# Two inner layer norms in a fixed order, scaled by token and then by feature, and a residual load that waits for x

## The chip, the cores and the metric

The kernel runs on one core of one Trainium2 chip. The engines named below are PE (TensorE, matrix products), DVE (VectorE), ACT (ScalarE), POOL (GpSimd) and SP (SyncE, which only issues DMAs here). The metric is the device time of one execution in microseconds (us); the median of the runs shown is 1940.43.

## What is computed

One layer over 256 tokens of width 2048 in 32-bit floats: a half-weight gated FFN, a mixer and a second half-weight FFN, each with a residual and a layer norm behind it.

```python
def layer_norm(x, gain, bias):
    mu = jnp.mean(xf, axis=-1, keepdims=True)
    var = jnp.mean(jnp.square(xf - mu), axis=-1, keepdims=True)
    return ((xf - mu) * lax.rsqrt(var + LN_EPS)).astype(x.dtype) * gain + bias

def swiglu_ffn(x, w_gate, w_up, w_down):
    return (jax.nn.silu(x @ w_gate) * (x @ w_up)) @ w_down
...
        x = layer_norm(DEEPNORM_ALPHA * x + FFN_RES_WEIGHT * swiglu_ffn(x, ...), ln1_gain, ln1_bias)
        mix = hybrid_mixer(x, positions, ...)
        x = layer_norm(DEEPNORM_ALPHA * x + mix, ln2_gain, ln2_bias)
        x = layer_norm(DEEPNORM_ALPHA * x + FFN_RES_WEIGHT * swiglu_ffn(x, ...), ln3_gain, ln3_bias)
```

The two inner norms are the first two: what they give is both the input of the next stage, needed with features on the partitions, and the residual of the next norm, needed with tokens on the partitions.

## The kernel before, in words

The 256 tokens are two tiles t of 128. Every matrix product is done with both operands split into a high and a low part. A weight unit is 128 x 2048 values, 1 MB: SP loads it into `raw` (three buffers), ACT casts the high part `h...` (L72, four buffers), DVE subtracts the low part `l...` (L73, four buffers), and PE multiplies: three matmuls of 512 columns for each k and t where the activation is the stationary side (`mm_t`, L94 to L98), or a pair of 512 and 256 columns where the weight is (`mm_f`, L90 to L92).

The stages run in this order. The first FFN has eleven hidden slices in chunks of 4, 4 and 3; its first gate and up products (`first`, L143 to L179) load x itself, in nine pieces `xr` on ACT's DMA queue (L163), split into `x_0` to `x_3` with four k each, and the first weights on SP (L167). The residual, x with tokens on the partitions, is loaded whole into `res[0]` and `res[1]` on POOL's queue (L180, L181). After each chunk `down` adds its product to `res` in four column slices n. In the last chunk (`f1dz_p`; in the mixer the output projection `opp`) the last slice n = 3 is computed for t = 0 and then for t = 1, and the norm follows.

`LN.finish(t)` (L282 to L297) does all on DVE: aggregate the moments, the root in 11 short operations on 128 x 1 values (`rsqrt`), then for each of four slices two passes over `res`: subtract the mean and multiply by the gain (L292), multiply by the root and add the bias (L294). `LN.turn(t, n)` transposes four 128 x 128 blocks on PE into a bank (L304), ACT casts the high part (L308), DVE subtracts the low part (L309). `LN.enter` (L311 to L324) runs the first product of the next stage (`v` of the mixer, `f2s` of the second FFN) over four units and both t, with the turns between. In trace rows the first inner norm is `f1n`, the second `mxn`, the last `f2n`; `res_75` and `res_76` are `res[0]` and `res[1]`. Behind the first norm come the mixer's `xb` products, 12 blocks of 16 pairs, and then `dtp` (L458).

Each engine runs its instructions in order. That order is made by a scheduler at build time, with its own idea of durations; only the loads on POOL that are marked `keep_in_program_order` are fixed among themselves. So the short steps of the root, the passes over `res` and the weight subtractions are mixed on DVE as the scheduler judged.

Of the kernel before, what the change touches and what calls it, by code (L numbers as in the profile page):

```python
# [8 lines left out]
F32 = mybir.dt.float32  # L9
# [37 lines left out]
def tile_layer(ctx, tc, aps, out):  # L47
# [19 lines left out]

    ident = const.tile([P, P], F32, name="ident")
    make_identity(nc, ident)

    def split(raw, hi, lo):
        nc.scalar.copy(out=hi, in_=raw)  # L72
        nc.vector.tensor_tensor(out=lo, in0=raw, in1=hi.bitcast(F32), op=ALU.subtract)  # L73

    def wunit(src, name, k, c, fine=1):
# [4 lines left out]
        if fine == 1:  # L80
            nc.sync.dma_start(out=raw[:, :n], in_=src)
        for j in range(fine):
            sl = slice(j * n // fine, (j + 1) * n // fine)
            if fine > 1:
                nc.sync.dma_start(out=raw[:, sl], in_=src[:, sl])
            split(raw[:, sl], hi[:, sl], lo[:, sl])
        return (hi[:, :n].rearrange("p (k c) -> p k c", c=c),
                lo[:, :n].rearrange("p (k c) -> p k c", c=c))

    def mm_f(ps, w, act, k, first, last):  # L90
        nc.tensor.matmul(ps, lhsT=w[0][:, k, :], rhs=act, start=first, stop=False)
        nc.tensor.matmul(ps[:, :T], lhsT=w[1][:, k, :], rhs=act[:, :T], start=False, stop=last)  # L92

    def mm_t(ps, act, t, w, k, first, last):  # L94
        ah, al = act(t)
        nc.tensor.matmul(ps, lhsT=ah, rhs=w[0][:, k, :], start=first, stop=False)  # L96
        nc.tensor.matmul(ps, lhsT=ah, rhs=w[1][:, k, :], start=False, stop=False)  # L97
        nc.tensor.matmul(ps, lhsT=al, rhs=w[0][:, k, :], start=False, stop=last)  # L98
# [7 lines left out]
    def fold(ps, name):  # L106
        lo = tmp(name + "c")
        nc.scalar.copy(out=lo, in_=ps[:, T:])
        s = tmp(name + "s")
        nc.vector.tensor_tensor(out=s, in0=ps[:, :T], in1=lo, op=ALU.add)  # L110
        return s

    def rsqrt(dst, hv, shape, name):
        y = dst
        nc.vector.tensor_scalar(out=y.bitcast(I32), in0=hv.bitcast(I32), scalar1=1, scalar2=None,
                                op0=ALU.arith_shift_right)
        nc.vector.tensor_scalar(out=y.bitcast(I32), in0=y.bitcast(I32), scalar1=-1,
                                scalar2=0x5EF759DF - (1 << 31), op0=ALU.mult, op1=ALU.add)
        t = small(name + "n", shape)
        for _ in range(3):  # L120
            nc.vector.tensor_tensor(out=t, in0=y, in1=y, op=ALU.mult)
            nc.vector.tensor_tensor(out=t, in0=t, in1=hv, op=ALU.mult)
            nc.vector.scalar_tensor_tensor(out=y, in0=t, scalar=1.5, in1=y,
                                           op0=ALU.subtract, op1=ALU.mult)
# [63 lines left out]
    nc.vector.tensor_copy(out=ustr_r, in_=ustr)  # L188
# [5 lines left out]
    tc.keep_in_program_order(nc.gpsimd.dma_start(out=rows, in_=aps["rows"].broadcast_to([P, 3, SH])))  # L194

# [18 lines left out]
    def turn(toks, name, hs):  # L214
        for b2 in range(2):
            pt = bank(f"{name}T{b2}")
            for bb in range(2):
                c0 = (2 * b2 + bb) * P
                for t in range(2):
                    nc.tensor.transpose(pt[:, bb * T + t * P:bb * T + (t + 1) * P], toks[t][:, c0:c0 + P], ident)  # L220
            hi = page(f"{name}h{b2}", F32R)
            lo = page(f"{name}l{b2}", F32R)
            nc.scalar.copy(out=hi, in_=pt)
            nc.vector.tensor_tensor(out=lo, in0=pt, in1=hi.bitcast(F32), op=ALU.subtract)
# [3 lines left out]
    def add_res(ps, t, n, start):  # L228
        r = res[t][:, n * NS:(n + 1) * NS]
        nc.vector.scalar_tensor_tensor(out=r, in0=r, scalar=ALPHA if start else 1.0, in1=ps,  # L230
                                       op0=ALU.mult, op1=ALU.add)

    def down(src, act, nu, name, start, ln=None, mid=None):
        for n in range(4):
            if ln is None or n < 3:
                pss = [bank(f"{name}p{n}{t}") for t in range(2)]
                for u in range(nu):
                    w = wunit(src(n, u), f"{name}{n}_{u}", 4, NS)
                    for k in range(4):
                        kk = 4 * u + k  # L240
                        for t in range(2):
                            mm_t(pss[t], act[kk], t, w, k, kk == 0, kk == 4 * nu - 1)
                    if mid is not None and n == 0 and u == 0:
                        mid()
                for t in range(2):
                    add_res(pss[t], t, n, start)
                    if ln is not None:
                        ln.stat(t, n)
                continue
            ws = [wunit(src(n, u), f"{name}{n}_{u}", 4, NS) for u in range(nu)]  # L250
            for t in range(2):
                ps = bank(f"{name}p{n}{t}")
                for u in range(nu):
                    if t == 1 and u == nu - 1:
                        ln.turn(0, 0)
                    for k in range(4):
                        kk = 4 * u + k
# [592 lines left out]
```

## Time and profile before

| | |
|---|---|
| median of 3 runs (lowest, highest) | 1940.43 us (1940.17, 1942.39) |
| profiled execution, its own time | 1940.14 us |
| its span in the trace | 1938.4 us |
| mean granted clock of PE | 0.989 |
| PE busy | 1888.9 us, 97% |
| DVE busy | 1046.6 us, 54% |
| ACT busy | 744.1 us, 38% |
| POOL busy | 59.7 us, 3% |

The span is the time between the first and the last instruction of the trace; 1.7 us of the execution lie outside. PE's share is the mean over stages: in the long ones it is full, and its idle time lies in a few places, which the views of waits, of windows and of single instructions show. The granted clock is given as a share of the full 2.4 GHz.

### The profile page before, as it was taken

The page shows a single profiled execution, that of the slowest core. Times are in us where ns is not written, and L with a number is a line of the kernel's source. Part 1 is how long each engine was busy: PE and PEld are TensorE (multiplying, and loading weights), DVE is VectorE, ACT ScalarE, POOL GpSimd, SP SyncE. Part 2 cuts the span into 40 slices and gives each one's busy share as a digit, 9 for nine tenths or more (in the row PEclk, how much of TensorE's full clock was granted, in tenths as well). Part 3 has the DMA queues.
Part 4 walks back from the last instruction along what each step waited for, and adds up shares of the span by engine and source line. Part 5 has one row for each costly group of instructions (what it writes and reads, how often), then busy time and mean ns, then how long its engine had stood idle before and what let it go on. Part 6 is the DMA issues. An engine that isn't in the chain of part 4 may idle for free.

```text
span 1938.4 us, 20670 instructions
## 1 busy us (share of the span) xinstructions
PE 1888.9 (97%) x8722; PEld 1570.8 (81%) x8722; DVE 1046.6 (54%) x1040; ACT 744.1 (38%) x592; POOL 59.7 (3%) x69
## 2 busy tenths in 40 slices
PE   7999999999999997999999997999999999999997
PEld 6888888888888886888888885888888888888885
DVE  5544444444444456667877656544444444444456
ACT  4433333334333332553335432443333334333331
POOL 2000000000000000002400000000000000000000
PEclk9999999999999998999999998999999999999998
DMA  8655555555556553544346552555555555556551
GB/s 296 231 185 186 194 195 195 178 191 195 195 203 218 191 195 120 195 174 160 145 152 209 204 196 88 215 183 187 195 195 195 186 186 193 195 192 226 190 196 65
DMA packets 53549, 363.04 MB, mean 187 GB/s; under 512 B 6224, under 2 KB 6496, under 8 KB 10960
## 3 DMA queue, kind: packets, MB, share of 16 engines
q1 hardware_dynamic: 49536, 350.25, 50.7%
q0 software_dynamic: 2624, 9.38, 1.4%
q10 hardware_dynamic: 1296, 2.10, 0.3%
q8 instruction: 68, 1.11, 0.2%
q14 instruction: 25, 0.20, 0.0%
HBM read 359.60 MB, written 2.10 MB: 187 GB/s over the span
## 4 chain that ended last, share of the span: by engine, by line
PE 95%; DVE 2%; DMA 2%; ACT 0%; issue 0%; DVEq 0%; ACTq 0%
PE f2u L97 4%; PE f2u L98 4%; PE f2u L96 4%; PE f1g L98 4%; PE f2g L98 4%; PE f2g L97 4%; PE f1g L97 4%; PE f1u L98 4%; PE f2g L96 4%; PE f1g L96 4%; PE f1u L97 4%; PE f1u L96 4%; PE f2d_p L97 3%; PE f2d_p L96 3%; PE f1d_p L97 3%; PE f1d_p L98 3%
## 5 line engine op out<-in xcount | busy, mean ns | idle before, releaser
L73 DVE TENSOR_TENSOR lf2u<-rf2u,hf2u 128x2048 fp32r<-128x2048 f32 x44 | 100.9, 2293 | 142.4 <-ACT hf2u L72 142.4
L73 DVE TENSOR_TENSOR lf1u<-rf1u,hf1u 128x2048 fp32r<-128x2048 f32 x40 | 91.7, 2293 | 121.5 <-ACT hf1u L72 121.5
L73 DVE TENSOR_TENSOR lf2g<-rf2g,hf2g 128x2048 fp32r<-128x2048 f32 x40 | 91.7, 2293 | 101.7 <-ACT hf2g L72 101.7
L73 DVE TENSOR_TENSOR lf1g<-rf1g,hf1g 128x2048 fp32r<-128x2048 f32 x40 | 91.6, 2292 | 97.7 <-ACT hf1g L72 97.7
L97 PE MATMUL f2u<-lf2u,mxnx 128*128 128x512 f32 x352 | 137.0, 389 | 1.1 <-DVE lf2u L73 1.1
L96 PE MATMUL f2u<-hf2u,mxnx 128*128 128x512 f32 x352 | 136.6, 389 | 0.7 <-ACT hf2u L72 0.7
L98 PE MATMUL f2u<-hf2u,mxnx 128*128 128x512 f32 x352 | 136.9, 389 | 0.0
L72 ACT CAST hf2u<-rf2u 128x2048 fp32r<-128x2048 f32 x44 | 84.1, 1910 | 118.0 <-PE f2g L98 105.1
L72 ACT CAST hf2g<-rf2g 128x2048 fp32r<-128x2048 f32 x40 | 76.5, 1913 | 131.9 <-PE f2u L98 101.6
L96 PE MATMUL f1g<-hf1g,x 128*128 128x512 f32 x320 | 125.3, 392 | 0.0
L96 PE MATMUL f2g<-hf2g,mxnx 128*128 128x512 f32 x320 | 125.3, 392 | 0.0
L98 PE MATMUL f2g<-hf2g,mxnx 128*128 128x512 f32 x320 | 124.6, 389 | 0.0
L72 ACT CAST hf1g<-rf1g 128x2048 fp32r<-128x2048 f32 x40 | 76.4, 1913 | 125.4 <-PE f1u L98 95.3
L98 PE MATMUL f1g<-hf1g,x 128*128 128x512 f32 x320 | 124.6, 389 | 0.0
L97 PE MATMUL f2g<-lf2g,mxnx 128*128 128x512 f32 x320 | 124.6, 389 | 0.0
L97 PE MATMUL f1g<-lf1g,x 128*128 128x512 f32 x320 | 124.5, 389 | 0.0
L96 PE MATMUL f1u<-hf1u,x 128*128 128x512 f32 x320 | 124.5, 389 | 0.0
L97 PE MATMUL f1u<-lf1u,x 128*128 128x512 f32 x320 | 124.5, 389 | 0.0
L98 PE MATMUL f1u<-hf1u,x 128*128 128x512 f32 x320 | 124.5, 389 | 0.0
L73 DVE TENSOR_TENSOR lf2d<-rf2d,hf2d 128x2048 fp32r<-128x2048 f32 x32 | 73.4, 2293 | 85.6 <-ACT hf2d L72 85.6
L73 DVE TENSOR_TENSOR lf1d<-rf1d,hf1d 128x2048 fp32r<-128x2048 f32 x32 | 73.4, 2293 | 85.6 <-ACT hf1d L72 85.6
L72 ACT CAST hf1u<-rf1u 128x2048 fp32r<-128x2048 f32 x40 | 76.4, 1910 | 105.0 <-PE f1g L98 104.2
(817 smaller groups left out, 4358.8 us busy)
## 6 DMA issues: line engine op xcount, KB each, us to landing
rf2u<-f_u SPq DMA_DIRECT2D x44, 1024.0 KB, 4.8
rf1g<-f_g SPq DMA_DIRECT2D x40, 1024.0 KB, 4.8
rf1u<-f_u SPq DMA_DIRECT2D x40, 1024.0 KB, 4.8
rf2g<-f_g SPq DMA_DIRECT2D x40, 1024.0 KB, 4.8
rf1d<-f_d SPq DMA_DIRECT2D x32, 1024.0 KB, 4.8
rf2d<-f_d SPq DMA_DIRECT2D x32, 1024.0 KB, 4.8
rop<-wout SPq DMA_DIRECT2D x16, 1024.0 KB, 4.8
rf1dz<-f_d SPq DMA_DIRECT2D x12, 1024.0 KB, 4.8
```

The costliest lines, as they stand in the source:

```text
L72: nc.scalar.copy(out=hi, in_=raw)
L73: nc.vector.tensor_tensor(out=lo, in0=raw, in1=hi.bitcast(F32), op=ALU.subtract)
L96: nc.tensor.matmul(ps, lhsT=ah, rhs=w[0][:, k, :], start=first, stop=False)
L97: nc.tensor.matmul(ps, lhsT=ah, rhs=w[1][:, k, :], start=False, stop=False)
L98: nc.tensor.matmul(ps, lhsT=al, rhs=w[0][:, k, :], start=False, stop=last)
```

## The change

1. **A fixed order.** A flag `strict` and a thin wrapper `Ordered` around the vector, scalar and tensor engines: whatever is issued while the flag is set keeps the order of the program among itself. All helper operations of the changed kernel carry the wrapper's line, L78.
2. **The inner norms.** `LN.close` replaces the last slice of `down`, `finish` and `enter`, and writes out the order by hand: matmuls, turns, weight units (`new`) and norm steps. After the root, `shift` makes -mean x root; `hat(t, n)` scales one slice of `res` on ACT by these two values per token. `turn` transposes it; four ACT operations of 128 x 128 apply gain and bias, which are now per partition (a new constant `lnp`), into a page `l1f` or `l2f`; cast and subtraction follow from that page. Gain and bias are applied to `res` itself afterwards, in 16 operations on DVE, outside the fixed order, with broadcast loads that are issued later.
3. **The last norm.** `close_last` keeps both passes on DVE, with the four first passes put between the steps of the root.
4. **The residual load.** It stands behind the constants on POOL's queue, and a copy of one value of the last slice of x into `res[t]` precedes each load, so that the load waits for that slice.

The core of the diff:

```diff
+    strict = [False]
+    class Ordered:
...
+                ins = fn(*args, **kw)
+                return tc.keep_in_program_order(ins) if strict[0] else ins
...
-    for t in range(2):
-        tc.keep_in_program_order(nc.gpsimd.dma_start(out=res[t], in_=aps["x"][t]))
...
+    lnp = const.tile([P, 4, KD], F32, name="lnp")
+    tc.keep_in_program_order(nc.gpsimd.dma_start(out=lnp, in_=aps["lnp"]))
+    for t in range(2):
+        tc.keep_in_program_order(nc.gpsimd.tensor_copy(out=res[t][:, :1], in_=x0_4[3][:, 3, 1, T - 1:].bitcast(F32)))
+        tc.keep_in_program_order(nc.gpsimd.dma_start(out=res[t], in_=aps["x"][t]))
...
+        def shift(self, t):
+            nb = self.nb[t] = small(f"{self.name}{t}nb", (P, 1))
+            vec.scalar_tensor_tensor(out=nb, in0=self.mv[t][:, 0:1], scalar=-1.0, in1=self.rs[t],
+                                     op0=ALU.mult, op1=ALU.mult)
+
+        def hat(self, t, n):
+            sca.activation(self.part(t, n), self.part(t, n), AF.Identity, bias=self.nb[t], scale=self.rs[t])
...
+            xf = page(f"{self.name}f{t}{n}")
+            for b in range(4):
+                c = 4 * n + b
+                sca.activation(xf[:, b * P:(b + 1) * P], pt[:, b * P:(b + 1) * P], AF.Identity,
+                               bias=lnp[:, 2 * self.idx + 1, c:c + 1], scale=lnp[:, 2 * self.idx, c:c + 1])
...
-            src = pt.rearrange("p (b c) -> p b c", b=4)
-            nc.scalar.copy(out=hi, in_=src)
-            nc.vector.tensor_tensor(out=lo, in0=src, in1=hi.bitcast(F32), op=ALU.subtract)
+            src = xf.rearrange("p (b c) -> p b c", b=4)
+            sca.copy(out=hi, in_=src)
+
+            def low():
+                vec.tensor_tensor(out=lo, in0=src, in1=hi.bitcast(F32), op=ALU.subtract)
+            return low
...
+        def close(self, piece, nu, name, start):
...
+            for _ in range(4 - nu):
+                new()()
+            strict[0] = True
+            pd = [bank(f"{name}p3{t}") for t in range(2)]
+            for u in range(nu):
+                piece(pd[0], 0, u)
+            add_res(pd[0], 0, 3, start)
+            self.stat(0, 3)
+            self.moments(0)
+            self.root(0)
+            self.shift(0)
+            piece(pd[1], 1, 0)
+            low = new()
+            self.hat(0, 0)
+            self.hat(0, 1)
+            low()
+            for u in range(1, nu - 1):
+                piece(pd[1], 1, u)
+                if u < nu - 2:
+                    new()()
+            piece(pd[1], 1, nu - 1, (0, 1))
+            low = self.turn(0, 0)
+            piece(pd[1], 1, nu - 1, (2, 3))
+            low()
+            new()()
+            low = self.turn(0, 1)
+            self.hat(0, 2)
+            low()
+            add_res(pd[1], 1, 3, start)
+            self.stat(1, 3)
+            self.moments(1)
...
+            enter(0, 0)
+            low = self.turn(0, 2)
+            self.hat(0, 3)
+            low()
+            new()()
+            self.root(1)
+            self.shift(1)
+            enter(0, 1)
+            low = self.turn(0, 3)
+            self.hat(1, 0)
+            self.hat(1, 1)
+            low()
+            enter(0, 2)
+            low = self.turn(1, 0)
+            self.hat(1, 2)
+            low()
...
+            strict[0] = False
+            self.affine()
+            for n in range(4):
+                for t in range(2):
+                    r = self.part(t, n)
+                    vec.tensor_tensor(out=r, in0=r, in1=self.gb[0][n], op=ALU.mult)
+                    vec.tensor_tensor(out=r, in0=r, in1=self.gb[1][n], op=ALU.add)
+            return pe
...
+                self.root(t, [lambda n=n: first(n) for n in range(4)])
```

The built order at three places. First, ACT's queue at the start, before (`xr` is a piece of x on its way in, `x_0` its high part, `hfirstu` and `hfirstg` the high parts of the first weights):

```order
12 L163 DMA xr_259<-xT 128x512
13 L163 DMA xr_261<-xT 128x512
14 L163 DMA xr_339<-xT 128x512
15 L163 DMA xr_341<-xT 128x512
16 L72 CAST x_0_77<-xr_111 128x2x256
17 L72 CAST hfirstu_88<-rfirstu_90 128x512
18 L72 CAST x_1_78<-xr_179 128x2x256
```

and the same stretch of ACT's queue after the change:

```order
12 L194 DMA xr_259<-xT 128x512
13 L78 CAST x_0_77<-xr_111 128x2x256
14 L194 DMA xr_261<-xT 128x512
15 L78 CAST hfirstu_88<-rfirstu_90 128x512
16 L194 DMA xr_339<-xT 128x512
17 L194 DMA xr_341<-xT 128x512
18 L78 CAST x_1_78<-xr_179 128x2x256
```

The casts of `x_0` and `hfirstu` have moved ahead of the last two or three loads of x.

Second, POOL's queue at the start after the change (before, the two `res` loads stood ahead of `ltri`, with no copies):

```order
10 L212 DMA ltri<-ltri 128x128
11 L214 DMA ustr<-ustr 128x128
12 L218 DMA par<-par 128x84
13 L220 DMA invf<-invf 128x1
14 L222 DMA rows<-rows 128x48
15 L225 DMA lnp<-lnp 128x64
...
20 L533 TENSOR_SCALAR n_4839<-ta 128x256
21 L534 TENSOR_SCALAR n_4839<-n_4839 128x256
22 L227 COPY res_75<-x_3_80 128x1
23 L228 DMA res_75<-x 128x2048
24 L227 COPY res_76<-x_3_80 128x1
25 L228 DMA res_76<-x 128x2048
```

The two loads have moved behind six constants, six rope operations and a copy each.

Third, DVE's queue in the first inner norm, before (`lv` is the low part of a unit of `v`; `f1n0rs`, `f1n0n` are the short steps of tile 0's root):

```order
246 L117 TENSOR_SCALAR f1n0rs<-f1n0rs 128x1
247 L73 TENSOR_TENSOR lv_4593<-rv_4594,hv_4592 128x2048
248 L121 TENSOR_TENSOR f1n0n<-f1n0rs 128x1
249 L122 TENSOR_TENSOR f1n0n<-f1n0n,f1n0hv 128x1
250 L73 TENSOR_TENSOR lv_4599<-rv_4600,hv_4598 128x2048
251 L123 SCALAR_TENSOR_TENSOR f1n0rs<-f1n0n,f1n0rs 128x1
252 L230 SCALAR_TENSOR_TENSOR res_76<-res_76,f1dz_p_4515 128x512
253 L121 TENSOR_TENSOR f1n0n<-f1n0rs 128x1
254 L73 TENSOR_TENSOR lv_4605<-rv_4606,hv_4604 128x2048
```

and DVE's queue behind tile 1's sum in the same norm after the change (`l1x` is the low part of a turned slice, `l11...` are tile 1's moments and root, in twelve steps of which the first three are shown):

```order
255 L78 SCALAR_TENSOR_TENSOR res_76<-res_76,f1dz_p_4448 128x512
256 L78 BN_STATS l1st_432<-res_76 128x6
257 L78 BN_AGGR l11mv<-l1st_432 128x2
258 L78 TENSOR_SCALAR l11hv<-l11mv 128x1
259 L78 TENSOR_TENSOR l1x_4439<-l1f_4606,l1x_4439 128x4x128
260 L78 TENSOR_TENSOR lv_4615<-rv_4616,hv_4614 128x2048
261 L78 TENSOR_SCALAR l11rs<-l11hv 128x1
262 L78 TENSOR_SCALAR l11rs<-l11rs 128x1
263 L78 TENSOR_TENSOR l11n<-l11rs 128x1
```

The steps of tile 0's root, mixed with weight subtractions before, stand together and ahead of all of this now; tile 1's stand behind the fourth weight unit's subtraction.

## Rows read from the trace of the kernel before

**Rows 1.** The page: busy time, and the chain that ended last
```profile
PE 1888.9 (97%) x8722; PEld 1570.8 (81%) x8722; DVE 1046.6 (54%) x1040; ACT 744.1 (38%) x592; POOL 59.7 (3%) x69
...
PE 95%; DVE 2%; DMA 2%; ACT 0%; issue 0%; DVEq 0%; ACTq 0%
```

**Rows 2.** PE's waits: waiting <- releaser: us in total, times, longest
```profile
PE mxnT L304 <- DVE res L294: 10.0, 1, 10.0
PE f1nT L304 <- DVE res L294: 9.5, 1, 9.5
...
PE first L96 <- ACT hfirstu L72: 4.6, 1, 4.6
```

**Rows 3.** Timeline of norm 1: start, duration, engine, operation, [idle before <- releaser]
```profile
736.58 0.69 DVE L230 SCALAR_TENSOR_TENSOR res<-res,f1dz_p 128x512 f32<-128x512 f32 x1 [3.92 <-PE f1dz_p L98]
...
739.30 1.91 ACT L72 CAST hv<-rv 128x2048 fp32r<-128x2048 f32 x1 [8.97 <-PE f1dz_p L98]
...
753.36 2.08 DVE L294 SCALAR_TENSOR_TENSOR res<-res,f1n0rs,f1ngb 128x512 f32<-128x512 f32 x3
```

**Rows 4.** Windows: length, PE, PEld, DVE, ACT, POOL busy, PEclk, DMA share, GB/s
```profile
16.00:22.00 6.00, 4.21 (x10) 3.24 (x11) 3.93 (x7) 4.18 (x8) 0.00 (x0) 0.50 1.02 391
...
745.00:749.00 4.00, 0.00 (x0) 0.00 (x0) 4.00 (x5) 1.63 (x1) 0.00 (x0) 1.00 0.88 334
...
750.00:759.00 9.00, 4.16 (x16) 3.46 (x17) 8.73 (x28) 1.25 (x3) 0.00 (x0) 0.50 0.38 149
...
775.00:778.00 3.00, 1.55 (x5) 0.82 (x6) 2.68 (x2) 1.75 (x4) 0.00 (x0) 1.00 0.00 0
...
1180.00:1192.00 12.00, 5.09 (x19) 4.33 (x20) 11.73 (x30) 1.92 (x4) 0.00 (x0) 0.50 0.43 159
```

**Rows 5.** Timeline of PE: marks of both inner norms, and distances of starts
```profile
744.09 0.39 PE L97 MATMUL f1dz_p<-lf1dz,f1t10h 128*128 128x512 f32 x1
744.31 0.39 PE L98 MATMUL f1dz_p<-hf1dz,f1t10l 128*128 128x512 f32 x1
...
790.25 0.40 PE L91 MATMUL xb<-f1nx,hxb 128*128 128x512 f32 x1
...
790.61 0.40 PE L91 MATMUL xb<-f1nx,hxb 128*128 128x512 f32 x1
...
853.14 0.84 PE L458 MATMUL dtp<-f1nx,wdt 128*32 128x512 f32 x3
...
1175.88 0.39 PE L98 MATMUL opp<-hop,mx 128*128 128x512 f32 x1
...
1245.02 1.03 PE L220 MATMUL f2t0T<-ident,f2t0a 128*128 128x128 f32 x8
```

**Rows 6.** Groups of ACT: count | busy us, mean ns | idle before, releaser
```profile
L308 ACT CAST f1nx<-f1nT 128x512 fp32r<-128x512 f32 x8 | 4.5, 588 | 13.9 <-PE f1nT L304 13.9
...
L707 ACT ACTIVATE onT<-ot,par 128x256 f32<-128x256 f32 x8 | 3.9, 562 | 3.5 <-PE ot L703 3.5
L535 ACT COPY btok<-cb 128x128 f32<-128x128 f32 x2 | 0.5, 264 | 0.0
```

**Rows 7.** Timeline of DVE: two short steps of the last norm's root
```profile
1930.04 0.16 DVE L122 TENSOR_TENSOR f2n1n<-f2n1n,f2n1hv 128x1 f32<-128x1 f32 x1
1930.23 0.16 DVE L123 SCALAR_TENSOR_TENSOR f2n1rs<-f2n1n,f2n1rs 128x1 f32<-128x1 f32 x1
```

**Rows 8.** Start: chain (start, us, what), ACT's timeline, DMA issue (KB, us to landing)
```profile
4.87 11.33 DMA xr<-xT
16.22 14.23 DMA xr<-xT
...
9.47 7.08 ACTq L163 DMA_DIRECT2D xr<-xT  x4
...
17.12 0.61 ACT L72 CAST hfirstu<-rfirstu 128x512 fp32r<-128x512 f32 x1
...
res<-x POOLq DMA_DIRECT2D x2, 1024.0 KB, 14.6
```

More of the change, by code (lines that the diff above doesn't have):

```diff
@@ L229, in add_res @@
         r = res[t][:, n * NS:(n + 1) * NS]
-        nc.vector.scalar_tensor_tensor(out=r, in0=r, scalar=ALPHA if start else 1.0, in1=ps,
+        vec.scalar_tensor_tensor(out=r, in0=r, scalar=ALPHA if start else 1.0, in1=ps,
                                        op0=ALU.mult, op1=ALU.add)
     def down(src, act, nu, name, start, ln=None, mid=None):
[L234 to L250, printed above, removed]
-            for t in range(2):
[L252 to L257, printed above, removed]
-                        mm_t(ps, act[kk], t, ws[u], k, kk == 0, kk == 4 * nu - 1)
-                add_res(ps, t, n, start)
-                ln.stat(t, n)
-                ln.finish(t)
@@ new lines, in down @@
+        for n in range(3 if ln else 4):
+            pss = [bank(f"{name}p{n}{t}") for t in range(2)]
+            for u in range(nu):
+                w = wunit(src(n, u), f"{name}{n}_{u}", 4, NS)
+                for k in range(4):
+                    kk = 4 * u + k
+                    for t in range(2):
+                        mm_t(pss[t], act[kk], t, w, k, kk == 0, kk == 4 * nu - 1)
+                if mid is not None and n == 0 and u == 0:
+                    mid()
+            for t in range(2):
+                add_res(pss[t], t, n, start)
+                if ln is not None:
+                    ln.stat(t, n)
@@ L263, in tile_layer, with piece, __init__ @@
+        if ln is None:
+            return None
+        ws = [wunit(src(3, u), f"{name}3_{u}", 4, NS) for u in range(nu)]
+        def piece(ps, t, u, ks=range(4)):
+            for k in ks:
+                kk = 4 * u + k
+                mm_t(ps, act[kk], t, ws[u], k, kk == 0, kk == 4 * nu - 1)
+        return ln.close(piece, nu, name, start)
     class LN:
[L264 to L265 removed]
+        def __init__(self, idx, name, nxt=None):
+            self.idx, self.name, self.nxt = idx, name, nxt
@@ new lines, in close_last, with first @@
+        def close_last(self, piece, nu, name, start):
+            strict[0] = True
+            for t in range(2):
+                ps = bank(f"{name}p3{t}")
+                for u in range(nu):
+                    piece(ps, t, u)
+                add_res(ps, t, 3, start)
+                self.stat(t, 3)
+                self.moments(t)
+                def first(n, t=t):
+                    r = self.part(t, n)
+                    vec.scalar_tensor_tensor(out=r, in0=r, scalar=self.mv[t][:, 0:1], in1=self.gb[0][n],
+                                             op0=ALU.subtract, op1=ALU.mult)
+                self.root(t, [lambda n=n: first(n) for n in range(4)])
+                for n in range(4):
+                    r = self.part(t, n)
+                    vec.scalar_tensor_tensor(out=r, in0=r, scalar=self.rs[t], in1=self.gb[1][n],
+                                             op0=ALU.mult, op1=ALU.add)
+                    nc.sync.dma_start(out=out[t][:, n * NS:(n + 1) * NS], in_=r)
+            strict[0] = False
@@ L372, in keep_v @@
                 vp = page(f"v{half}{t}")
-                nc.scalar.copy(out=vp, in_=vps[half][t])
+                sca.copy(out=vp, in_=vps[half][t])
                 vts[half].append(vp)
```

342 lines of the change are left out of this document (183 added, 159 removed).

## The prediction

> **What bounds the kernel now.** I read the chain that ended last first: 95% of it is TensorE (PE), 2% VectorE (DVE), 2% DMA [rows 1]. So the time is PE's work plus the places where PE stands still, and only those places can be won. PE's waits name three large ones [rows 2]: 9.5 and 10.0 us where the first transposition of an inner normalisation waits for the scaled residual, and 4.6 us near the start, where a matmul waits for a cast of a weight.
>
> Normalisation 1. The sum of token tile 0 is complete at 736.58, yet its last scaling starts on DVE only at 753.36 [rows 3]. DVE was not idle: its queue mixes the short steps of the square root with both tiles' scalings and three 2.2 us weight subtractions, and it was busy 4.00 of 4.00 us while PE stood [rows 4]. What PE loses altogether comes from marks. From the last `f1dz_p` matmul (744.31) to the first `dtp` matmul (853.14) are 108.8 us [rows 5]. The work in it is 97 matmuls at .227, 192 `xb` pairs at .353 (both the distance of two starts [rows 5]) and 32 transposes, 8 fours at about .35: 22.0 + 67.8 + 2.8 = 92.6. **16.2 us are lost.** Normalisation 2, from 1175.88 to `f2t0T` at 1245.02: 69.1 less 217 x .227 + 2.8 = 52.0, so **17.1 lost**. Part of that is the clock: it still stood at 1.00 early in the pause and was 0.50 (1.2 GHz) for 9 and 12 us around the restart, in which PE was busy 4.16 and 5.09 us [rows 4]; half of those is lost, 2.1 and 2.5.
>
> Start. The chain runs through DMAs of x: one is under way 4.87 to 16.20, the next is issued at 16.22, the moment the earlier one has landed, and takes 14.23 [rows 8]. ScalarE's (ACT's) queue is held in its four DMA issues for 7.08 us from 9.47, so the cast of `hfirstu`, which waits for no data of its own, runs at 17.12 [rows 8]. In that time the two 1 MB residual loads, 14.6 us each, share the DMA engines, whose share is 1.02 at 391 GB/s in 16:22 [rows 4, 8]. PE stood 4.6 us and then ran at 0.50 until about 22: 4.21 busy us, 2.1 lost [rows 2, 4].
>
> **The change part by part.** *Residual load.* On POOL it moves behind the constants, the first rope operations and a copy that waits for the last slice of x; behind it wait the last two rope operations and the gain and bias loads, which the mixer needs hundreds of us later. The residual itself is first read after four hidden slices, each 192 matmuls: 4 x 192 x .227 = 174 us, so its landing costs nothing. It now competes with the last weight units of the first projection, from about 26 us on; a unit has 48 matmuls, 10.9 us, against 1 MB at 391 GB/s, 2.7, so I cost that at nothing; without that slack it would be 1 to 2 us. On ACT, the cast of x and that of `hfirstu` now stand ahead of the DMA issues that were held. Won: the 4.6 us wait and the 2.1 of the clock, and about 1 us of the later wait for the x that landed at 30.45 [rows 8]; against it small new waits of 1 to 2 us where first-projection subtractions stand behind rope steps on DVE. Ends 4 and 7; I take **6.1**, near the upper end, since the two rows that make the gain are both removed.
>
> *Normalisations 1 and 2.* Sixteen scalings of 128x512 leave DVE's path in each (and 16 multiplies and adds of about .69 [rows 3] come after it, for the residual alone: 11 us of DVE beside 68 us of `xb` matmuls or an FFN projection. DVE is busy 54% over all [rows 1], so I cost them at nothing; uncovered they would be 11). Added to ACT's path: 8 `hat` of 128x512, 32 small scalings of 128x128, 8 casts as before. Prices: the cast .588; a scaling with two per-partition operands at 128x256 .562; a copy of 128x128 .264 [rows 6]. The small scaling lies between the last two; back to back I take .35 for it (ends .26 and .45), for `hat` .65 (ends .5 and .8, the cast and DVE's .69 being near).
>
> I walk the new order with these prices in the old trace's time. Tile 0 sums at 736.58 and has its half variance at 738.3; then twelve dependent short steps at .195 [rows 7] with nothing between: the factors stand at 740.7. `hat`(0,0) follows the weight cast of 739.30 [rows 3], at 741.1, and ends at 741.8. Its transposition stands at 743.18 in PE's order: **no wait, the 9.5 us are gone.** What comes instead:
> - turn (0,0): T, four small scalings, cast, subtraction end at 746.7, while PE has six matmuls and a turn to do: .8 + .3 waited.
> - T(0,2): `hat`(0,2) stands on ACT behind a weight cast and the whole of turn (0,1): 1.5. T(0,3): .4.
> - T(1,0): on DVE the fourth weight unit's subtraction, whose cast runs 753.8 to 755.8, stands ahead of tile 1's twelve short steps. They end at 758.1 + 2.3 = 760.4, `hat`(1,0) at 761.1; PE was through at 757.0: 4.1. This is the largest wait left.
> - the first `xb` unit, whose buffer comes free late: .9.
>
> Sum 7.9 or 8.0 (in normalisation 2, by the same walk, 7.7), against 16.2 and 17.1 lost before. Then the clock: pauses of 4.6, 9.5 and 10.0 us were followed by 0.50, while in 775:778, PE 1.55 us busy with two pauses near 1 us, it stayed at 1.00 [rows 2, 4]. The 4.1 us pause is nearer to the first, so I count a fall, 2.1 to 2.5 less what the waits behind it absorb: 1.9. Won: 16.2 - 7.9 - 1.9 = **6.4** and 17.1 - 7.7 - 1.9 = **7.5**. Bounds: with the small scaling at .45, 2.0 and 1.6 less; at .26, 1.0 more each; `hat` at either end, .6 either way.
>
> The Trainium skill has a price for the small scaling ("ScalarE: Activation LUTs", What ACT_TABLE_LOAD costs): 186 ns and .833 ns per element, 93 ns for each per-partition operand, 93 ns overlapped back to back. For 128 elements and two operands that is an estimate of .386 apart, and .705 for `hat`; at 128x256 it would say .585 where the row has .562. By the page the sum would be 1.6 us smaller over both normalisations.
>
> *Last normalisation.* Its four first scalings now stand between the short steps instead of ahead of them and fill four waits of .195 less an issue of about .07 [rows 7]: .26 a tile; both tiles lie on the end. **0.5.**
>
> **The rivals.** *A, the clock stays up* in both 4.1 us pauses: 3.8 us more won, 1916. For it: the pauses are shorter than any after which it fell. Against: 4.6 is near. *B, ACT is dearer than I take it,* small scalings .45 or more and `hat` .8: 3.6 + 1.2 lost and the pauses still there: 1925. For it: 40 new ACT instructions in each chain; the .562 row halved is more than .26. The skill's rule speaks for it ("ScalarE: Activation LUTs", Rules for kernel authors: add and multiply belong on VectorE, not ScalarE); in this trace ACT was busy 1.63 of the 4.00 us in which DVE was full [rows 4]. *C, the start gives little:* the x loads stay a chain, each issued when an earlier one lands, and a later weight or x takes the wait's place; won 1 rather than 6: 1925. For it: two DMA issues still stand ahead of the second x cast. Against: 2 MB less in the same stretch. *D, slower: the clock stays at 0.50 through the whole chain of turns,* since each turn brings a new small pause. Place: the 96 entry matmuls of each normalisation, .43 instead of .23 each: 19 us, and .35 more for each of 8 turns, 3; less some 5 of pauses that a slower PE absorbs, 17 each: 1916 + 34 = 1950. It decides, being slower than before by what can be told, when more than about 85 of the 96 matmuls in both run at half clock; against it, the clock was back 5 to 6 us after each restart [rows 4] although PE was busy under half of that time. *E, the order is not what runs,* or its cover for subtractions fails elsewhere (the multiplies of the residual in front of `xb` subtractions): 11 us a normalisation at most, 1938 to 1941. The order of the built kernel shows the rows where I put them, so little. *F, better than walked:* .26 small scalings, full clock, start 7: 1912.
>
> **How the numbers follow.** 6.1 + 6.4 + 7.5 + 0.5 = 20.5. The profiled execution took 1940.14 (span 1938.4 and 1.7 outside), the median is 1940.43: 1919.6 and 1919.9. I predict **1920**. Chances: this case 1917 to 1923 .44; A .13; B .16; C .14; F .06; D .03; E .04. The range 1913 to 1928 takes in A, B and C and their mixtures; D, E and part of F are left out. The measurement tells apart about 0.2%, 3.9 us: faster .93, same .04 (E), slower .03 (D).
>
> **What would show it.** Right: PE's waits name no 9 us wait for a scaled residual; the largest in each normalisation is about 4 us at the first transposition of tile 1, ended by ACT's `hat`, behind DVE's short steps; from the last `f1dz_p` to `dtp` 102.4 us, from the last `opp` to `f2t0T` 61.6. The start's wait for `hfirstu` is gone, the first transposition of the FFN comes about 6 us earlier, the residual loads are issued near 26 to 31. In the last stretch, the end follows the last matmul by .26 less. Wrong: a granted clock of 1.00 throughout the normalisations (A), small scalings at .45 apart (B), a wait of over 3 us before 30 us (C), granted 0.50 over more than 10 us of dense matmuls (D).

## The result, and the profile after

The changed kernel takes 1920.79 us (median of 4 runs, 1920.13 to 1921.6) against 1941.41 for the kernel before in the same comparison: a ratio of 0.9894, interval 0.9877 to 0.9911, or 20.6 us less, where 1920 was forecast. The executions of the kernel before lie in two groups, near 1939.9 (17 of all 28 on record) and near 1942.2, so that a median of a few falls anywhere between them; by the mean of all 28, 1940.8, the gain is 20.0. The profiled execution of the changed kernel took 1921.3 with a span of 1919.5, 18.9 less than the span of the profiled one of before. What follows divides these 18.9.

The page of the changed kernel, the chain that ended last, and the waits of PE (all of L78, the wrapper's line):

```profile
PE 95%; ACT 2%; DVE 2%; DMA 1%; issue 0%; POOL 0%; SPq 0%; DVEq 0%
```

```profile
PE first L78 <- ACT hfirstg L78: 7.3, 2, 5.8
PE l2T L78 <- ACT res L78: 5.3, 3, 3.8
PE l1T L78 <- issue: 3.8, 1, 3.8
PE l1T L78 <- ACT res L78: 1.5, 2, 1.3
PE first L78 <- DVE lfirstu L78: 0.8, 1, 0.8
```

The waits of 9.5 and 10.0 us [rows 2] are gone; each norm has one of 3.8 instead, and shorter ones. The wait of 4.6 us for `hfirstu` is gone too; 1.5 for `hfirstg` and 0.8 for `lfirstu` are new in the start (the 5.8 in the first line is the wait for the very first data, which both kernels have).

The marks of rows 5 in PE's timeline of the changed kernel:

```profile
739.70 0.40 PE L78 MATMUL f1dz_p<-hf1dz,f1t10l 128*128 128x512 f32 x1
...
841.04 0.40 PE L78 MATMUL dtp<-l1x,wdt 128*32 128x512 f32 x1
...
1164.25 0.40 PE L78 MATMUL opp<-hop,mx 128*128 128x512 f32 x1
...
1226.65 1.03 PE L78 MATMUL f2t0T<-ident,f2t0a 128*128 128x128 f32 x8
```

PE does the same matmuls between these marks; only the first turn of each norm, .35 us, now lies ahead of the first and third mark, which the table takes into account (739.70 counts as 739.35).

| stretch | before | after | won | forecast |
|---|---|---|---|---|
| start to the last `f1dz_p` | 744.3 | 739.35 | 5.0 | 6.1 |
| to the first `dtp` (norm 1) | 108.8 | 101.7 | 7.1 | 6.4 |
| to the last `opp` | 322.7 | 322.9 | -0.1 | 0 |
| to `f2t0T` (norm 2) | 69.1 | 62.75 | 6.4 | 7.5 |
| to the end of the span | 693.4 | 692.85 | 0.5 | 0.5 |
| sum | | | 18.9 | 20.5 |

The long wait left in norm 1, from ACT's, DVE's and PE's timelines:

```profile
748.99 1.89 ACT L78 CAST hv<-rv 128x2048 fp32r<-128x2048 f32 x1
750.92 2.29 DVE L78 TENSOR_TENSOR lv<-rv,hv 128x2048 fp32r<-128x2048 f32 x1 [1.82 <-ACT hv L78]
753.13 0.15 DVE L78 TENSOR_SCALAR l11rs<-l11hv 128x1 int32<-128x1 int32 x1
...
755.24 0.16 DVE L78 SCALAR_TENSOR_TENSOR l11nb<-l11mv,l11rs 128x1 f32<-128x1 f32 x1
...
755.44 1.52 ACT L78 ACTIVATE res<-res,l11nb,l11rs 128x512 f32<-128x512 f32 x2 [2.46 <-DVE l11nb L78]
...
756.35 1.09 PE L78 MATMUL l1T<-ident,res 128*128 128x128 f32 x4 [3.81 <-issue]
```

This is the chain that was walked: the fourth unit's cast, its subtraction on DVE, tile 1's twelve short steps behind it, `hat`, the turn. The waits view names no releaser for PE here ("issue"); the rows do. The clock, in windows (columns as in rows 4):

```profile
14.00:17.00 3.00, 2.06 (x8) 1.41 (x9) 2.68 (x5) 2.92 (x6) 0.23 (x1) 1.00 1.01 406
...
752.00:756.00 4.00, 0.54 (x3) 0.12 (x1) 3.62 (x14) 1.45 (x3) 0.00 (x0) 1.00 0.42 124
757.00:758.00 1.00, 1.00 (x5) 0.90 (x4) 0.00 (x0) 0.52 (x2) 0.00 (x0) 0.50 0.36 148
...
1180.00:1182.00 2.00, 1.13 (x5) 1.14 (x6) 0.56 (x1) 1.52 (x2) 0.00 (x0) 0.50 0.94 397
1184.00:1188.00 4.00, 4.00 (x16) 3.22 (x15) 0.69 (x1) 1.61 (x5) 0.00 (x0) 0.71 0.00 0
```

(0.71 is a mean over a stretch that is partly at 0.50 and partly at 1.00.) At the start it no longer falls. In the norms it does, late in the 3.8 us wait, for about 3 us in norm 1 and 7 in norm 2.

### The profile page after: what moved, and what is told of

Its sections match the earlier page's. It is cut to its first block, busy times and chain, and to the rows that moved or that the text cites. A ratio compares the mean times of both kernels' runs of the same rounds, so it can differ in the third digit from the quotient of the medians.

```text
span 1919.5 us, 20769 instructions
## 1 busy us (share of the span) xinstructions
PE 1885.5 (98%) x8722; PEld 1566.5 (82%) x8722; DVE 1046.7 (55%) x1044; ACT 778.2 (41%) x672; POOL 60.9 (3%) x72
## 4 chain that ended last, share of the span: by engine, by line
PE 95%; ACT 2%; DVE 2%; DMA 1%; issue 0%; POOL 0%; SPq 0%; DVEq 0%
PE f2u L78 12%; PE f1g L78 11%; PE f2g L78 11%; PE f1u L78 11%; PE f1d_p L78 9%; PE f2d_p L78 9%; PE opp L78 4%; PE xb L78 3%; PE f1dz_p L78 3%; PE f2dz_p L78 3%; PE g L78 2%; PE z L78 2%; PE first L78 1%; PE v L78 1%; PE v0e L78 1%; DVE res L78 1%
## 5 line engine op out<-in xcount | busy, mean ns | idle before, releaser
L78 PE MATMUL f2u<-hf2u,l2x 128*128 128x512 f32 x704 | 218.8, 389 | 0.0
L78 PE MATMUL f1g<-hf1g,x 128*128 128x512 f32 x640 | 201.5, 391 | 0.0
L78 PE MATMUL f2g<-hf2g,l2x 128*128 128x512 f32 x640 | 201.2, 391 | 0.0
L78 PE MATMUL f1u<-hf1u,x 128*128 128x512 f32 x640 | 198.6, 389 | 0.0
L78 DVE TENSOR_TENSOR lf2u<-rf2u,hf2u 128x2048 fp32r<-128x2048 f32 x44 | 100.9, 2292 | 125.2 <-ACT hf2u L78 125.2
L78 DVE TENSOR_TENSOR lf1u<-rf1u,hf1u 128x2048 fp32r<-128x2048 f32 x40 | 91.7, 2292 | 122.3 <-ACT hf1u L78 122.3
L78 PEld LDWEIGHTS f2u<-hf2u,l2x 128*128 128x128 f32 x704 | 132.1, 188 | 27.3
L78 DVE TENSOR_TENSOR lf1g<-rf1g,hf1g 128x2048 fp32r<-128x2048 f32 x40 | 91.6, 2292 | 101.5 <-ACT hf1g L78 101.5
L78 DVE TENSOR_TENSOR lf2g<-rf2g,hf2g 128x2048 fp32r<-128x2048 f32 x40 | 91.6, 2292 | 98.7 <-ACT hf2g L78 98.7
L78 PEld LDWEIGHTS f1u<-hf1u,x 128*128 128x128 f32 x640 | 120.1, 188 | 24.9
L78 PEld LDWEIGHTS f1g<-hf1g,x 128*128 128x128 f32 x640 | 120.2, 188 | 24.8
L78 PEld LDWEIGHTS f2g<-hf2g,l2x 128*128 128x128 f32 x640 | 120.1, 188 | 24.6
L78 PE MATMUL f2u<-lf2u,l2x 128*128 128x512 f32 x352 | 137.0, 389 | 0.2 <-DVE lf2u L78 0.2
L78 ACT CAST hf2g<-rf2g 128x2048 fp32r<-128x2048 f32 x40 | 76.5, 1913 | 131.4 <-PE f2u L78 98.9
L78 ACT CAST hf2u<-rf2u 128x2048 fp32r<-128x2048 f32 x44 | 84.1, 1911 | 110.6 <-PE f2g L78 104.7
L78 ACT CAST hf1g<-rf1g 128x2048 fp32r<-128x2048 f32 x40 | 76.4, 1913 | 125.0 <-PE f1u L78 95.3
L78 PE MATMUL f1g<-lf1g,x 128*128 128x512 f32 x320 | 124.6, 389 | 0.0
L78 PE MATMUL f2g<-lf2g,l2x 128*128 128x512 f32 x320 | 124.6, 389 | 0.0
L78 PE MATMUL f1u<-lf1u,x 128*128 128x512 f32 x320 | 124.5, 389 | 0.0
L78 DVE TENSOR_TENSOR lf2d<-rf2d,hf2d 128x2048 fp32r<-128x2048 f32 x32 | 73.4, 2293 | 85.6 <-ACT hf2d L78 85.6
L78 DVE TENSOR_TENSOR lf1d<-rf1d,hf1d 128x2048 fp32r<-128x2048 f32 x32 | 73.4, 2293 | 85.6 <-ACT hf1d L78 85.6
L78 ACT CAST hf1u<-rf1u 128x2048 fp32r<-128x2048 f32 x40 | 76.4, 1910 | 106.3 <-PE f1g L78 105.5
```

The source lines that it names most:

```text
L78: ins = fn(*args, **kw)
```

## Experiments

Theory: the start gains because 2 MB of residual are out of the way of the first x and weights; the norms gain by the order written by hand, which puts tile 0's root together; what is left there is tile 1's root behind a weight subtraction and the fall of the clock that follows. Rivals: the start gains through ACT's queue order; the norms gain because the scaling went to ACT. Medians below are compared with 1920.79 for the changed kernel; "before" ran at 1940.0 to 1940.7 beside them.

### The residual load alone, undone and done

Undone in the changed kernel:

```diff
+    for t in range(2):
+        tc.keep_in_program_order(nc.gpsimd.dma_start(out=res[t], in_=aps["x"][t]))
     ltri = const.tile([P, P], F32, name="ltri")
...
-        tc.keep_in_program_order(nc.gpsimd.tensor_copy(out=res[t][:, :1], in_=x0_4[3][:, 3, 1, T - 1:].bitcast(F32)))
-        tc.keep_in_program_order(nc.gpsimd.dma_start(out=res[t], in_=aps["x"][t]))
```

> The changed kernel with the residual load alone put back: first on POOL's queue, without the copy that makes it wait. Theory (the start's gain comes from this load alone): the wait for hfirstu comes back, the first f1t0T stands 5.4 us later than in the changed kernel, both inner norms are as in the changed kernel, so about 1926.2. Rival (the start's gain comes from the new order of ACT's queue or of the constants, and the residual's 2 MB do not matter): within 1 us of the changed kernel, about 1920.8.

1927.25 us (1925.46 to 1927.7), 6.5 slower than the changed kernel, where 5.4 was expected. It has the old wait again, and in the norms the waits of the changed kernel:

```profile
PE first L78 <- ACT hfirstu L78: 4.3, 1, 4.3
```

The reverse, the kernel before with only this edit:

> The kernel before with the residual load alone moved behind the last slice of x. Theory: the start gains the same 5.4 us (4.9 once the first FFN is through), the norms keep their waits of 9.5 and 10.0 us, about 1936. Rival (the parts do not add up, since a later start only moves the same waits): 1940 to 1941.

1934.54 us (ratio 0.9973, 0.9962 to 0.9984), 6.2 faster than before; in the profiled run the first transposition of the FFN starts at 59.86 against 65.60, and the norms are untouched:

```profile
PE mxnT L305 <- DVE res L295: 10.0, 1, 10.0
PE f1nT L305 <- issue: 9.5, 1, 9.5
```

By means of the runs instead of medians the two differences are 6.1 and 5.5. So the load is worth 5.5 to 6.5 us, with either norm, and the rest of the change about 13.5 to 14.5.

### Traffic or the order of ACT's queue

The moved load also changed where the scheduler puts the loads of x in ACT's queue. Two runs hold that queue by hand, one with the residual early and the order of after, one with the residual late and the order of before (`d` issues a load of x, `c` splits one into its high and low part, `s` a weight slice; DVE's subtractions in these splits are held with the casts). This is the line in which the two runs differ:

```diff
-    [d(2, 2), d(3, 0), d(3, 2), c(0, 2), s(1, 1)]   # order of before
+    [c(0, 2), d(2, 2), s(1, 1), d(3, 0), d(3, 2)]   # order of after
```

> The changed kernel with the residual loaded first, as before, but ACT's queue at the start held in the order of the changed kernel by hand (the casts of x_0 and hfirstu ahead of the last three loads of x). It tells the two effects of the moved load apart: 2 MB less among the DMAs, and the other order of ACT's queue that came with it. Theory (the traffic is the larger part): the cast of hfirstu is early, but the weights and x of k 2 and 3 land at 17 to 20 us as in the kernel before, PE waits there instead; 1 to 2 us better than with the residual early and the old order (1927.2), so 1925 to 1926. Rival (the held queue is the larger part): 1921 to 1922.

1927.37 us: no better than with the old order (1927.25), where 1 to 2 us were expected. `hfirstu` is cast at 12.44 instead of 17.12 [rows 8], and PE then stands for the next data, which lands no earlier:

```profile
12.44 0.61 ACT L78 CAST hfirstu<-rfirstu 128x512 fp32r<-128x512 f32 x1
...
16.74 0.62 ACT L78 CAST x<-xr 128x512 fp32r<-128x512 f32 x1 [3.68 <-DMA xr<-xT]
```

```profile
17.93 1.22 PE L78 MATMUL first<-hfirstg,x 128*128 128x512 f32 x2 [2.81 <-ACT hfirstg L78]
```

> The changed kernel, residual late, with ACT's queue at the start put back by hand to the order of the kernel before (all loads of x ahead of the casts of x_0 and hfirstu). Theory (traffic is the larger part): the queue is held only until about 13.6 us, when an earlier x has landed, PE waits about 3 us for hfirstu and not again for hfirstg; 1 to 2 us slower than the changed kernel, 1922 to 1923. Rival (the held queue is the larger part): 4 us or more slower, 1925 to 1926.

1921.55 us, 0.8 slower, less than the 1 to 2 expected. The queue is held, but for 4.48 us instead of 7.08 [rows 8], since the x it waits for lands earlier:

```profile
9.21 4.48 ACTq L182 DMA_DIRECT2D xr<-xT  x4
```

The traffic is the cause; the queue order is worth under 1 us.

### The load at its new place, without the wait

```diff
-        tc.keep_in_program_order(nc.gpsimd.tensor_copy(out=res[t][:, :1], in_=x0_4[3][:, 3, 1, T - 1:].bitcast(F32)))
         tc.keep_in_program_order(nc.gpsimd.dma_start(out=res[t], in_=aps["x"][t]))
```

> The changed kernel with the residual load at its new place behind the constants, but without the copy that makes it wait for the last slice of x: it is issued near 5.5 us, 3 us later than before the change and 22 us earlier than in the changed kernel. ACT's queue keeps the order of the changed kernel. Theory (what counts is that the 2 MB are out of the way until the first x and weights have landed, so the wait makes the gain): most of the start's loss returns, 3 to 5 us slower than the changed kernel, 1924 to 1926. Rival (the place behind the constants is enough, since the first transfers are issued by then): 1921 to 1922.

1931.19 us (1929.79 to 1931.89): 10.4 slower than the changed kernel, and 4 slower than with the load first. The direction was right, the size missed. Issued at 5.48 and 8.00, the load meets the x and weights of k 2 and later. PE waits four times behind the very first data, and the clock falls three times, to 0.50 in 17:20, 28:30 and 38:40 (the first is shown; columns as in rows 4):

```profile
PE first L78 <- ACT hfirstg L78: 9.8, 3, 5.7
...
PE first L78 <- DVE lfirstu L78: 2.3, 1, 2.3
PE first L78 <- DVE lfirstg L78: 0.9, 1, 0.9
```

```profile
17.00:20.00 3.00, 3.00 (x8) 2.18 (x9) 1.20 (x2) 0.60 (x2) 0.00 (x0) 0.50 1.01 412
```

These waits are 5.0 us more than those of the changed kernel (7.3 against 2.3, without the 5.7 or 5.8 for the very first data), and three falls of the clock, which the changed kernel does not have there, cost 5.1 (busy time times 1 less the granted share, by windows of 1 us). The expectation counted on the old loss coming back, not on a second round of waits. The wait, not the place in the queue, makes the gain.

### The order alone, with the arithmetic of before

The run also loads gain and bias ahead of the norms, as the kernel before does; the diff here is its core.

```diff
-            sca.activation(self.part(t, n), self.part(t, n), AF.Identity, bias=self.nb[t], scale=self.rs[t])
+            vec.scalar_tensor_tensor(out=r, in0=r, scalar=self.mv[t][:, 0:1], in1=self.gb[0][n],
+                                     op0=ALU.subtract, op1=ALU.mult)
+            vec.scalar_tensor_tensor(out=r, in0=r, scalar=self.rs[t], in1=self.gb[1][n],
+                                     op0=ALU.mult, op1=ALU.add)
...
-                sca.activation(xf[:, b * P:(b + 1) * P], pt[:, b * P:(b + 1) * P], AF.Identity,
...
-            src = xf.rearrange("p (b c) -> p b c", b=4)
+            src = pt.rearrange("p (b c) -> p b c", b=4)
...
-                    vec.tensor_tensor(out=r, in0=r, in1=self.gb[0][n], op=ALU.mult)
```

> The changed kernel with its order written by hand, but with the arithmetic of the kernel before: both passes of the inner norms on DVE (L292 and L294 before), no scaling by feature after the transposition, the cast straight from the transposed bank, no second application to the residual. Theory (the gain in the norms is made by the order): every turn is 1.5 us shorter on ACT, every slice 1.4 us longer on DVE; the waits before the third and fourth turn of tile 0 grow to about 1.6 and 0.9, the one before tile 1 stays 3 to 4, 1919 to 1923. Rival (the gain is made by scaling on ACT by token and feature): the waits for scaled residual return, 9 us and more in all per norm, 1930 or more.

1921.50 us (1920.98 to 1921.92), 0.7 from the changed kernel. The waits have other sizes and the same sum:

```profile
PE l2T L78 <- DVE res L78: 4.9, 3, 2.8
PE l1T L78 <- issue: 2.9, 1, 2.9
PE l1T L78 <- DVE res L78: 1.6, 2, 1.1
PE v0e L78 <- DVE l1x L78: 1.1, 2, 0.8
```

Against the kernel before with the load moved (1934.54) that is 13.0 us. So the gain in the norms is that of the fixed order. Scaling on ACT by token and feature, the part that the change is named for, gives nothing by itself. Which part of the order makes the gain for tile 0 (the root's steps together on DVE, the turns among PE's matmuls, ACT's queue) no run took apart.

### Scaling by token on DVE

```diff
-            sca.activation(self.part(t, n), self.part(t, n), AF.Identity, bias=self.nb[t], scale=self.rs[t])
+            vec.tensor_scalar(out=self.part(t, n), in0=self.part(t, n), scalar1=self.rs[t], scalar2=self.nb[t],
+                              op0=ALU.mult, op1=ALU.add)
```

> The changed kernel with the scaling by token on DVE (one operation of 128x512 with both factors) in place of ACT, at the same place of the order written by hand. Theory (what gains is the fixed order, with the root's steps together; ACT is the fuller queue in the turns): the waits of 1.3 and 0.2 us before the third and fourth turn of tile 0 shrink, the 3.8 us one stays, 2 to 3 us faster than the changed kernel, about 1918. Rival (the gain comes from taking the scaling off DVE): DVE's subtractions come later by 0.7 us for each scaling and PE waits for them, 3 to 6 us slower than the changed kernel.

1917.75 us (1916.83 to 1919.63), 3.0 faster, part of it the clock, which in the profiled run did not fall in norm 1. The operation takes .54 there against .81 on ACT:

```profile
L78 DVE TENSOR_SCALAR res<-res,l10rs,l10nb x4: 539/541/546, 735.6 to 747.6; 128x512 f32<-128x512 f32 x4
```

The longest wait came down from 3.8 to 3.2 in both norms, which was not expected, and the 0.2 us wait went; the 1.3 us wait before the third turn stayed, since DVE's subtraction now stands ahead of it.

### Tile 1's root ahead of the fourth weight unit

```diff
-            new()()
             self.root(1)
             self.shift(1)
+            new()()
```

> The changed kernel with tile 1's root and shift put ahead of the fourth weight unit in the order written by hand. Theory (the wait of 3.8 us before the first turn of tile 1 is made by that unit's subtraction standing ahead of the root on DVE, and the fall of the clock by that wait): the factors come 2.2 us earlier and the wait is 1.2 to 1.6 us, the granted clock stays at 1.00 in both norms, each norm gains 2.3 and the 1.6 to 2.7 us that half clock costs there: about 8 us, 1912 to 1914. Rival (ACT is the bound there: scaling, turn and cast take its time whatever DVE does): the wait stays over 3 us and the time within 2 us of 1920.8. Second rival (the clock falls for another reason than this wait): the wait goes, the clock still falls, 1916.

1912.18 us (1912.04 to 1912.47), 8.6 faster than the changed kernel: two lines exchanged. The factors stand 2.2 us before the subtraction ends, the wait is 1.3 and the clock stays up in both norms:

```profile
PE l2T L78 <- ACT res L78: 2.6, 3, 1.3
PE l1T L78 <- ACT res L78: 1.5, 2, 1.3
PE l1T L78 <- issue: 1.3, 1, 1.3
```

```profile
752.00:756.00 4.00, 2.73 (x14) 2.01 (x14) 2.00 (x2) 3.82 (x9) 0.00 (x0) 1.00 0.36 100
...
1170.00:1175.00 5.00, 3.83 (x20) 2.97 (x19) 4.23 (x11) 4.93 (x9) 0.00 (x0) 1.00 0.04 10
```

Two waits shorter by 2.5 are 5.0; the rest of the spans' 9.2 us agrees with the 4.3 that the two falls cost in the profile of the changed kernel.

### The wait kept, PE busy in it

```diff
             enter(0, 2)
+            junk = bank(f"{ename}junk")
+            for _ in range(14):
+                ten.matmul(junk, lhsT=act[8](0)[0], rhs=ws[2][0][:, 0, :], start=True, stop=True)
             low = self.turn(1, 0)
```

> The changed kernel with 14 matmuls of 512 columns into a bank that nobody reads (3.2 us at full clock) put into PE's queue ahead of the first turn of tile 1, in both inner norms, where PE waits 3.8 us. The wait's end is not moved. Theory (the half clock behind that wait is made by PE standing still there, and costs 1.6 and 2.7 us): the clock stays at 1.00, 3 to 4.5 us faster than the changed kernel, 1916.5 to 1918. Rival (the fall costs nothing, since the chain behind it waits anyway, or it comes for another reason): 1920 to 1922.

1917.47 us (1917.13 to 1917.62), 3.3 faster with 28 useless matmuls more. The turn of tile 1 starts as it did, and the clock behind it is 1.00:

```profile
752.25 3.33 PE L78 MATMUL v0junk<-hv,l1x 128*128 128x512 f32 x14
756.23 0.63 PE L78 MATMUL l1T<-ident,res 128*128 128x128 f32 x4 [0.64 <-issue]
```

```profile
756.00:760.00 4.00, 3.77 (x21) 3.26 (x22) 0.69 (x1) 3.68 (x8) 0.00 (x0) 1.00 0.31 131
...
1178.00:1182.00 4.00, 3.41 (x18) 2.57 (x17) 0.83 (x3) 3.63 (x8) 0.00 (x0) 1.00 0.50 209
```

So PE's standing still makes the fall, and the fall costs about 3.3 of the two norms' time beyond the waits.

### A faster version

Scaling by token on DVE, all four slices of tile 0 behind its root, tile 1's sum ahead of the third weight unit, its root and first scaling ahead of the fourth:

```diff
             self.hat(0, 1)
+            self.hat(0, 2)
+            self.hat(0, 3)
...
             low()
+            add_res(pd[1], 1, 3, start)
+            self.stat(1, 3)
             new()()
             low = self.turn(0, 1)
-            self.hat(0, 2)
             low()
-            add_res(pd[1], 1, 3, start)
-            self.stat(1, 3)
             self.moments(1)
...
-            self.hat(0, 3)
             low()
-            new()()
             self.root(1)
             self.shift(1)
+            self.hat(1, 0)
+            new()()
```

> Aimed at a faster version: the changed kernel with scaling by token on DVE, all four of tile 0 at once behind its root, tile 1's sum ahead of the third weight unit, tile 1's root and first scaling ahead of the fourth. Theory: no wait before the third and fourth turn of tile 0; what is left is ACT's chain of four small scalings and a cast per turn (0.4 and about 0.5 us) and the fourth unit's subtraction (about 1 us); waits of 2 to 3 us in a norm against 3.6 with the root first alone; 1909 to 1911. Rival (ACT's chain of turns is the bound by now): the waits move to the casts and the time stays at 1912.

1910.45 us (1910.25 to 1910.73), ratio to before 0.9845 (0.9830 to 0.9859): 10.3 faster than the changed kernel and the fastest of all runs. No turn waits for its residual any more; what is left is about 2 us a norm in waits of 0.6 and less.

With ACT's queue at the start fixed by hand on top of it, the last two loads of x behind the casts for k 2 and 3:

> The faster order of both inner norms (run e6_root_hats, 1910.5) with ACT's queue at the start also fixed by hand: the last two loads of x behind the casts for k 2 and 3. Theory (the 1.5 us wait for hfirstg in the start comes from ACT being held in those two DMA issues for 3 us): the wait shrinks to under 1 us, 0.5 to 1 us faster, 1909.5 to 1910. Rival (the data lands no earlier): 1910.5.

1912.14 us: a miss, 1.7 slower. There was little to win: in the profile of e6_root_hats, with the queue held for 3.27 us, the wait for `hfirstg` was only 0.3 (5.9 in all, less the 5.6 for the very first data), and here it is 1.3. With the queue free, the cast of x ahead of `hfirstg` runs at 13.23 instead of 13.68, so it had waited for x itself more than for the queue. And on DVE the last x now comes later, and three rope steps, the first of them waiting for POOL, stand ahead of it and of `lfirstu`, as the scheduler placed them:

```profile
26.03 1.34 DVE L78 SCALAR_TENSOR_TENSOR th<-n,th 128x256 f32<-128x256 f32 x3 [1.23 <-POOL n L549]
27.30 0.68 DVE L78 TENSOR_TENSOR x<-xr,x 128x512 fp32r<-128x512 f32 x1
```

PE's wait for `lfirstu` grew from 0.8 to 2.1, and behind it the clock fell, which costs 1.7:

```profile
28.97 0.50 PE L78 MATMUL first<-lfirstu,x 128*128 128x512 f32 x1 [2.06 <-DVE lfirstu L78]
```

```profile
30.00:33.00 3.00, 3.00 (x9) 2.33 (x8) 3.00 (x6) 0.74 (x2) 1.30 (x2) 0.50 0.88 344
```

An order fixed on one queue leaves the scheduler to mend the others, for better or worse.

## Why the prediction was right, point by point

**The start, 6.1 forecast.** About right, near the upper end: 5.5 to 6.5 by the two runs that move the load alone; 5.0 in the profiled pair, 5.5 up to the first transposition of the FFN (65.60 to 60.15). Two of its terms were a little off: PE's wait behind the x that landed at 30.45 was 0.45 in the kernel before, not about 1, and the new waits came to 2.3, where 1 to 2 were allowed. The reason given was half right. Two causes were named, traffic and the held queue, "since the two rows that make the gain are both removed"; the runs show that the first is nearly all of it. In the changed kernel the residual lands in 6.7 us instead of 14.6 [rows 8]. The new waits are 1.5 and 0.8; the second is where it was put, behind a rope step, and the first behind a cast of x whose queue is held again:

```profile
10.65 2.98 ACTq L194 DMA_DIRECT2D xr<-xT  x2
13.67 0.62 ACT L78 CAST x<-xr 128x512 fp32r<-128x512 f32 x1 [2.41 <-DMA xr<-xT]
```

Run e9_start_too, which frees the queue there, has this cast at 13.23: about 0.4 us of the 1.5 is the queue, the rest is x on its way.

**Norms, 6.4 and 7.5.** 13.9 forecast, 13.5 found in the profiles. The walk had the waits at their places and a little long: 7.9 and 7.7 against 6.2 and 5.9 in the waits view (the longest 4.1 against 3.8, before the third turn 1.5 against 1.3).

That the sum came out so closely is in part luck. By the prediction's own count of work (92.6 and 52.0) PE still loses 9.1 and 10.7 us; the waits are 6.2 and 5.9 of it, the clock 1.6 and 2.7, and 1.3 and 2.1 are neither. The kernel before had such a rest too, 1.9 and 1.6 of its 16.2 and 17.1. The prediction compared the whole loss before with waits and clock alone after, and so put the rest at nothing; this error of 3.4 and the waits that were 3.5 too long cancel. Part of the rest shows behind each turn, where the first matmul takes .32 to the next start (738.45 to 738.77) instead of .227.

The prices held:

```profile
742.60 1.50 ACT L78 ACTIVATE l1f<-l1T,lnp 128x128 f32<-128x128 f32 x4
```

```profile
L78 ACT ACTIVATE l1f<-l1T,lnp x32: 444/456/467, 738.7 to 771.1; 128x128 f32<-128x128 f32 x32
...
L78 ACT ACTIVATE res<-res,l10nb,l10rs x4: 802/810/813, 736.0 to 748.3; 128x512 f32<-128x512 f32 x4
```

Four small scalings in 1.50, one of them .456, are .35 apart, as taken; `hat` is .81, and .70 apart (two in 1.52), where .65 was taken. The estimate from the Trainium skill ("ScalarE: Activation LUTs", What ACT_TABLE_LOAD costs) was .386 and .705: high for the first, right for the second.

**The clock.** 1.9 was taken for each fall. From busy time at less than full clock (busy time times 1 less the granted share, by windows of 1 us) it cost 1.6 in norm 1 and 2.7 in norm 2 of this profile, and norm 2 falls short of its forecast by that. One profile does not settle the term, though. Four other runs (e1_res_early, s1_early_free, s2_late_held, e7_no_copy) have the same order in both norms and the same wait of 3.7 to 3.8, and there a fall cost from 1.4 to 3.0; the mean of all ten is 1.9, and the mean gain of the two norms over the five profiles is 6.7 and 7.3. The longest of these falls, in norm 1 of s1_early_free:

```profile
762.00:767.00 5.00, 5.00 (x14) 4.09 (x15) 0.69 (x1) 3.37 (x7) 0.00 (x0) 0.50 0.19 80
```

The run with PE kept busy gets 3.3 back for the two. That the fall would come was right; rival A is refuted for these two waits.

**The last norm, 0.5:** 0.5. It all shows behind the last matmul, from whose start to the end of the span are 14.6 us before and 14.1 after; the sign that was named for that stretch, .26, counted only one of the two tiles.

**Rivals.** B (ACT dearer) is refuted by the prices, though its ground was sound. The rule that it cited from the Trainium skill ("ScalarE: Activation LUTs", Rules for kernel authors), that multiply and add belong on VectorE (DVE), is borne out here by .54 against .81 and by the 3.0 us of run e4_hat_dve. C is refuted by the two runs on the load. D and E did not happen. The ground against D was misread: the 4.16 busy us of 750:759 [rows 4] all lie behind the restart at 754.17, so PE was busy most of the time until the clock was back, not under half of it. As for E, the 16 late multiplies and adds lie beside PE's work with no wait in its view but the 0.5 for `lxb`, against 1.1 before. What the prediction did not ask was whether the scaling on ACT was needed for the gain at all: it costed the change as one, and the run with both passes on DVE, 1921.50, shows that the order carries it.

## What to carry to other kernels

Where a scheduler mixes a chain that PE waits for with work that only needs to be done sometime, fix the order of that chain first, and test the order apart from the new arithmetic: here the order was worth about 13 us and the arithmetic nothing. Then look in the new order for the same fault: tile 1's root stood behind a weight subtraction, and exchanging two lines gave another 8.6. A load that nobody needs soon should wait for the loads that PE needs at once, by a dependence and not by a place in a queue.

## What the runs showed of the hardware that was not expected

- A residual load issued at 5.5 and 8.0 us cost the start more than the same 2 MB issued from 2.3 us on (1931.2 against 1927.3): it then met the transfers that PE needed next.
- After a wait of 2 to 4 us the granted clock does not follow from the length of the wait. With 2.65 us at the start (run s2_late_held) it stayed at 1.00; with 3.2 us (run e4_hat_dve) it stayed in norm 1 and fell in norm 2, where PE had waited equally long. It also fell behind 2.9 (run e5_dve_passes, norm 1) and, at the start, behind 2.3 (run e7_no_copy) and 2.1 (run e9_start_too); in that last case PE was running again for 0.7 us before the clock fell. In run e7_no_copy it fell behind two waits of 0.8 and 0.9 us in succession, where two pauses near 1 us before left it at 1.00 (775:778 [rows 4]). What decides it is open:

```profile
756.00:760.00 4.00, 4.00 (x20) 3.13 (x19) 1.79 (x4) 2.74 (x8) 0.00 (x0) 1.00 0.13 53
...
1175.00:1180.00 5.00, 2.57 (x8) 2.24 (x9) 3.54 (x14) 1.42 (x4) 0.00 (x0) 0.71 0.58 210
```

(windows of run e4_hat_dve behind the wait of each norm).

- An operation of 128x512 with two per-partition factors takes .54 us on DVE and .81 on ACT; DVE's two-tensor form took .69 [rows 3].
